# Token groups of 4, 4, 3, 3, 3 instead of 3, 4, 4, 3, 3, with packed small inputs, decay masks a tile at a time and row factors ahead of their spread

## Chip, cores, metric

The kernel runs on one core of one Trainium2 chip. The metric is the device time of one execution in microseconds. Shorter is better. Besides the timed runs there is one execution under the hardware profiler, whose trace gives all rows below.

## What is computed

One layer of a hybrid encoder for 2,048 prompt tokens and 8 x 16 sample tokens, in float32, with a model width of 1,024:

```python
h = rmsnorm(x, norm_mix_pre)
P = h @ w_in                                  # q, k, v, z, b, a, B, C, H
q, k, v = silu(causal_dwconv(P[qkv], 4 taps)); q, k = l2norm(q), l2norm(k)
beta = sigmoid(b);  g = -exp(a_log) * softplus(a + dt_bias)
o = gated_delta_rule(q, k, v, g, beta, S0)    # chunks, a unit-triangular solve in each
o = rmsnorm(o, gdn_norm_w) * silu(z)
y = B * causal_dwconv(C * H, 3 taps)
x = x + rmsnorm(concat(o, y) @ w_o, norm_mix_post)
x = x + rmsnorm(swiglu(rmsnorm(x, norm_ffn_pre)), norm_ffn_post)
```

## The kernel before

The 17 tiles of 128 tokens (tile 16 holds the sample tokens) are worked through in three phases. The first, up to some 905 us of the trace, does the input projection and the delta rule; the second the output projection; the third the feed-forward part. Each float32 product is made of three matmuls: both factors are split into a rounded high part and its remainder (`hi`/`lo` for the input, `wh`/`wl` for a weight).

**Groups and blocks.** In the first phase tiles are taken in five groups (`GROUPS`); a group's columns, 384 or 512, are the width of its matmuls. For each group 28 weight blocks of 128 columns run (`BLOCKS`: k, v, q, z by head, then C, H, B), in the order of `SEQS`. A block is 24 matmuls (L298) into a PSUM bank `dbank`; `finish_block` evacuates it on DVE or ACT (`R`, `sz`, `cs`, `u`, `yo`), and for k, q and v runs a convolution of three taps on DVE (L302). In group 0 each weight block is loaded raw by SP's queue (`wr`, L276), cast on ACT (L277), its remainder taken on DVE (L278) and the pair stored back to memory (`wsplit`, L283); later groups mostly load the stored pair.

**Who sets the order.** TensorE's order is written out by hand: `plan` puts small steps into `events`, at times counted in thirds of a block (3 x place of the block, plus 0, 1 or 2), and the loop over blocks runs those of a third behind its matmuls. The other engines' instructions are ordered by the compiler's scheduler; each engine then runs its own in that order. The numbers of `plan` stand in `PLAN`, by the group's number of tiles, with an entry of its own for group 0: rates, sums, decay, mask, norms, pairs, load, store, the four levels, chunks.

**The delta rule's steps.** `gate_rates`, `gate_sums` and `gate_decay` make the decays; `decay_mask` adds mask and row term for all tiles of a group (L523); `pair_keys` multiplies keys by keys into `AU`. `solve_load` copies the diagonal blocks into `pk` (ACT) and transposes them into `As` (DVE, L569); `solve` makes 31 steps of two DVE instructions each (L578, L580), spread over the plan; `solve_store` transposes the result into `utd` (L585, L586). `level_a` to `level_d` put the block inverses together: level a's matmuls (L600) read `utd`. Then `chunk` takes tile after tile through the state `S`, in four steps.

**The next group's rows.** `x_rows_load` (SP, L228) loads a tile's rows, `x_rows` (ACT, L235) takes their sums of squares; `x_spread` makes the factors (DVE, GpSimd), multiplies them onto a diagonal (DVE, L204) and spreads them over the partitions by a matmul with ones (L207). Group 0 can't wait for that: its first three blocks run on the plain input, and the factors come in at the evacuation (`rb`). Its prologue splits the input (L215, L216), squares it (L874, L875, L878), runs the three blocks, the sums of squares (L888), 16 gate matmuls (L153), then the spread, whose result `rb` is needed by the first evacuation (L309).

**Small inputs.** The identity and ones (`cst`), then the norm vectors (`vec`, 17 numbers a partition) are loaded by ACT's queue at the start; nine more loads (the masks, convolution weights, caches, gate numbers) follow from the same queue behind the first splits.

## Time and profile before

| what | us |
| --- | --- |
| timed runs: 2511.01, 2507.51, 2511.68; median | 2511.01 |
| the profiled execution, its own time | 2506.84 |
| its span, first to last instruction | 2505.1 |
| TensorE busy in it | 2455.0 |
| DVE busy | 1610.7 |
| ACT busy | 1059.6 |

A view by stages gives for each stretch the busy time of each engine, then the granted clock of TensorE (1.00 is full), the busy share of the DMA engines and GB/s. A row of the timeline is start, length, engine (SPq and ACTq are DMA issues), line, operation, out<-in, shapes, count, and in brackets how long the engine had been idle and for whom. A row of groups ends with busy time, mean ns of one, and the idle time ahead of them. A matmul's length covers its way through the array; neighbours overlap, so its cost is the distance from start to start.

### The profile page before, as it was taken

The page shows a single profiled execution, that of the slowest core. Times are in us where ns is not written, and L with a number is a line of the kernel's source. Part 1 is how long each engine was busy: PE and PEld are TensorE (multiplying, and loading weights), DVE is VectorE, ACT ScalarE, POOL GpSimd, SP SyncE. Part 2 cuts the span into 40 slices and gives each one's busy share as a digit, 9 for nine tenths or more (in the row PEclk, how much of TensorE's full clock was granted, in tenths as well). Part 3 has the DMA queues.
Part 4 walks back from the last instruction along what each step waited for, and adds up shares of the span by engine and source line. Part 5 has one row for each costly group of instructions (what it writes and reads, how often), then busy time and mean ns, then how long its engine had stood idle before and what let it go on. Part 6 is the DMA issues. An engine that isn't in the chain of part 4 may idle for free. (4 is left out here: it accounts for less than half of the span.)

```text
span 2505.1 us, 39369 instructions
## 1 busy us (share of the span) xinstructions
PE 2455.0 (98%) x14366; PEld 2247.2 (90%) x14366; DVE 1610.7 (64%) x3032; ACT 1059.6 (42%) x2355; POOL 579.5 (23%) x656
## 2 busy tenths in 40 slices
PE   8999999999999999999999999999999999999997
PEld 7898888889999988889999999999999987887786
DVE  5976645645656555878888754455555564677698
ACT  5556445445435343444443422223333345333343
POOL 1101011011011001135665400000000055455563
PEclk9999999999999999999999999999999999999999
DMA  7855555456667556688876878778898843333365
GB/s 275 310 213 193 211 198 193 175 170 231 242 225 240 200 183 211 209 297 319 292 269 238 290 250 277 264 242 267 291 308 280 259 147 122 93 126 126 128 224 184
DMA packets 282499, 561.91 MB, mean 224 GB/s; under 512 B 26109, under 2 KB 174785, under 8 KB 265025
## 3 DMA queue, kind: packets, MB, share of 16 engines
q1 hardware_dynamic: 161200, 483.52, 56.1%
q10 hardware_dynamic: 121104, 75.88, 9.7%
q8 instruction: 113, 1.85, 0.3%
q14 instruction: 82, 0.66, 0.1%
HBM read 400.62 MB, written 158.70 MB: 223 GB/s over the span
## 5 line engine op out<-in xcount | busy, mean ns | idle before, releaser
L1268 PE MATMUL fbank<-xh,fw 128*128 128x384 f32 (+1 forms) x3696 | 897.8, 326 | 5.9 <-ACT m L1300 2.6
L298 PE MATMUL dbank<-hi,w 128*128 128x384 f32 (+1 forms) x2240 | 672.0, 368 | 8.8 <-ACT w L277 6.2
L1268 PEld LDWEIGHTS fbank<-xh,fw 128*128 128x128 f32 x3696 | 651.0, 188 | 7.5 <-ACT m L1300 3.0
L1268 PE MATMUL fbank<-xl,fw 128*128 128x384 f32 (+1 forms) x1848 | 601.9, 326 | 0.0
L298 PEld LDWEIGHTS dbank<-hi,w 128*128 128x128 f32 x2240 | 416.8, 190 | 47.8 <-ACT w L277 6.2
L1434 PE MATMUL fbank<-dw,as 128*128 128x512 f32 x1884 | 442.6, 393 | 7.5 <-DVE as L1418 2.6
L1434 PEld LDWEIGHTS fbank<-dw,as 128*128 128x128 f32 x1884 | 353.6, 188 | 90.3 <-DVE acc L1393 3.9
L298 PE MATMUL dbank<-lo,w 128*128 128x384 f32 (+1 forms) x1120 | 402.3, 359 | 1.1 <-DVE lo L216 1.1
L1268 PEld LDWEIGHTS fbank<-xl,fw 128*128 128x128 f32 x1848 | 346.9, 188 | 0.0
L1418 POOL TENSOR_TENSOR as<-ar,as 128x256 fp32r<-128x256 f32 (+1 forms) x207 | 186.8, 913 | 226.3 <-ACT as L1415 223.8
L298 PEld LDWEIGHTS dbank<-lo,w 128*128 128x128 f32 x1120 | 212.9, 190 | 18.7 <-DVE lo L216 1.7
L1393 DVE TENSOR_TENSOR acc<-acc,fbank 128x512 f32<-128x512 f32 x248 | 166.3, 682 | 96.1 <-PE fbank L1434 81.9
L1415 ACT CAST as<-ar 128x256 fp32r<-128x256 f32 (+1 forms) x288 | 118.5, 428 | 184.6 <-PE fbank L1434 133.9
L1118 POOL TENSOR_TENSOR dw<-dr,dw 128x512 fp32r<-128x512 f32 x48 | 70.0, 1467 | 520.3 <-ACT dw L1116 520.3
L1243 ACT CAST fw<-rg 128x512 fp32r<-128x512 f32 x124 | 77.4, 624 | 193.8 <-PE fbank L1268 153.1
L302 DVE SCALAR_TENSOR_TENSOR acc<-R,cw,acc 128x384 f32<-128x384 f32 (+2 forms) x180 | 121.6, 678 | 53.2 <-ACT acc L332 44.2
L1313 DVE TENSOR_TENSOR c<-u,fbank 128x384 f32<-128x384 f32 (+1 forms) x66 | 34.9, 529 | 109.9 <-PE fbank L1268 109.9
L1311 ACT ACTIVATE m<-fbank 128x384 f32<-128x384 f32 (+1 forms) x66 | 31.3, 474 | 124.4 <-PE fbank L1268 117.3
L1309 DVE TENSOR_TENSOR m<-m,m 128x384 f32<-128x384 f32 (+1 forms) x44 | 23.1, 525 | 88.8 <-ACT m L1302 88.7
L1244 POOL TENSOR_TENSOR fw<-rg,fw 128x512 fp32r<-128x512 f32 x44 | 71.0, 1614 | 37.0 <-ACT fw L1243 34.7
L324 POOL COPY hist<-R 128x3 f32<-128x3 f32 x60 | 17.0, 283 | 254.5 <-ACT R L307 201.9
L1302 ACT COPY m<-fbank 128x384 f32<-128x384 f32 (+1 forms) x66 | 30.6, 463 | 82.9 <-PE fbank L1268 57.8
(362 smaller groups left out, 3550.6 us busy)
## 6 DMA issues: line engine op xcount, KB each, us to landing
w<-wsplit SPq DMA_DIRECT2D x105, 1024.0 KB, 5.1
fw<-fsplit SPq DMA_DIRECT2D x188, 512.0 KB, 4.7
fsplit<-fw SPq DMA_DIRECT2D x94, 512.0 KB, 3.9
partd<-pt ACTq DMA_DIRECT2D x88, 384.0 KB, 6.6
rg<-in_w_gu SPq DMA_DIRECT2D x62, 512.0 KB, 3.8
wsplit<-w SPq DMA_DIRECT2D x28, 1024.0 KB, 4.9
ar<-partd SPq DMA_DIRECT2D x48, 384.0 KB, 3.3
wr<-in_w_in SPq DMA_DIRECT2D x34, 512.0 KB, 5.8
```

Of the source, the lines that this page charges most:

```text
L298: T.matmul(ps[:, :c], l[:, k, :], r[k][:, :c], start=(k == 0 and r is hi and l is wh), stop=(k == KD - 1 and l is wl))
L302: r = V.scalar_tensor_tensor(acc, raw(d), w[:, d:d + 1], acc, op0=ALU.mult, op1=ALU.add)
L1118: e.tensor_tensor(out=w[1], in0=v, in1=w[0].bitcast(F32), op=ALU.subtract)
L1243: A.copy(w[:, 0], v)
L1244: e.tensor_tensor(out=w[:, 1], in0=v, in1=w[:, 0].bitcast(F32), op=ALU.subtract)
L1268: T.matmul(ps, w_[:, c], b_[k][:, :hw], start=(first and k == 0 and ci == 0), stop=(k == KH - 1 and ci == 2), skip_group_check=not first)
L1311: A.activation(sg0, b1, AF.Silu)
L1313: V.tensor_add(c21, u2, b3)
L1393: V.tensor_add(dst, dst, ps)
L1415: ins = A.copy(a[:, 0, :n], v)
L1418: e.tensor_tensor(out=a[:, 1, :n], in0=v, in1=a[:, 0, :n].bitcast(F32), op=ALU.subtract)
L1434: T.matmul(ps, a[:, x_, q * P:(q + 1) * P], w[y_], start=(start and q == 0 and ci == 0), stop=(q == c - 1 and ci == 2), skip_group_check=True)
```

## The change

Group 0 gets four tiles and group 2 three. `SEQS` takes the v blocks of group 0 earlier, and `PLAN` now has an entry for each group. The convolution, gate and scaling numbers are packed by the host into `vec` (147 numbers a partition), which is loaded first; the masks get a tile of their own and, like the caches, are loaded from SP's queue. Stores of split weights wait until four weight blocks are loaded. The squares of the prologue come behind the second weight block's cast and remainder, two of them on DVE and six on ACT. The factors' diagonal is a step of its own (`diagonal`, `x_factors`), three thirds ahead of the spread; in the prologue the third block's last nine matmuls and eight of the gate matmuls stand ahead of the spread and eight behind it. Rows are loaded every four thirds from 43 on. `decay_mask` and `decay_scale` run a tile at a time. In `level_a` the copies to the diagonals stand behind the two copies that level b reads; from group 1 on four of them are on DVE. Where chunk steps would run far into the next group, the last start is held at its second third.

```diff
-GROUPS = [[0, 1, 2], [3, 4, 5, 6], [7, 8, 9, 10], [11, 12, 16], [13, 14, 15]]
+GROUPS = [[0, 1, 2, 3], [4, 5, 6, 7], [8, 9, 10], [11, 12, 16], [13, 14, 15]]
...
-SEQS = ([0, 12, 1, 13, 2, 14, 3, 15, 8, 16, 9, 17, 10, 18, 11, 19, 4, 20, 5, 21, 6, 7, *range(22, 28)],
+SEQS = ([0, 12, 1, 13, 2, 14, 3, 15, 8, 16, 9, 17, 10, 4, 11, 5, 18, 6, 19, 7, *range(20, 28)],
         [*range(0, 4), *range(8, 12), *range(12, 16), *range(4, 8), *range(16, 28)])
-PLAN = {0: (13, 18, 20, 26, 34, 35, 39, 53, (64, 67, 69, 71), 73),
-        3: (6, 12, 15, 22, 17, 27, 31, 47, (51, 54, 57, 59), 61),
-        4: (6, 12, 15, 20, 17, 24, 29, 42, (45, 48, 50, 52), 55)}
+PLAN = {0: (13, 19, 21, 25, 31, 32, 36, 49, (61, 63, 65, 67), 68),
+        1: (6, 12, 15, 19, 17, 24, 29, 42, (45, 48, 50, 52), 55),
+        2: (6, 12, 15, 21, 17, 27, 31, 47, (52, 55, 58, 60), 62),
+        3: (6, 12, 15, 21, 17, 27, 31, 47, (53, 56, 59, 61), 63),
+        4: (6, 12, 15, 21, 17, 27, 31, 47, (52, 55, 58, 60), 62)}
...
-    cst = const.tile([P, 904], F32, name="cst")
+    cst = const.tile([P, 256], F32, name="cst")
     half_eye = consts[:, 904:]
-    nc.scalar.dma_start(out=cst[:, 0:256], in_=consts[:, 0:256])
-    late = lambda: nc.scalar.dma_start(out=cst[:, 256:], in_=consts[:, 256:904])
-    ident, ones, tri_p, tri_s, blk_s, smask, neg_p, neg_s = (cst[:, a:b] for a, b in CONSTS.values())
-    vec = const.tile([P, 17], F32, name="vec")
+    ident, ones = cst[:, 0:128], cst[:, 128:256]
+    vec = const.tile([P, 147], F32, name="vec")
     nc.scalar.dma_start(out=vec, in_=vecs)
+    nc.scalar.dma_start(out=cst, in_=consts[:, 0:256])
...
+        masks = gp.tile([P, 648], F32, name="masks")
+        tri_p, tri_s, blk_s, smask, neg_p, neg_s = (masks[:, a - 256:b - 256] for a, b in list(CONSTS.values())[2:])
...
-        def spread(r, n):
+        def diagonal(r, n):
+            rg = xbuf()
+            V.tensor_mul(rg[:, :n * P].rearrange("p (t i) -> p t i", t=n), ident.unsqueeze(1).broadcast_to([P, n, P]),
+                         r.unsqueeze(2).broadcast_to([P, n, P]))
+            return rg
+
+        def spread(rg, n):
             c = n * P
-            rg = xbuf()
-            V.tensor_mul(rg[:, :c].rearrange("p (t i) -> p t i", t=n), ident.unsqueeze(1).broadcast_to([P, n, P]),
-                         r.unsqueeze(2).broadcast_to([P, n, P]))
             ps = tbank()
             T.matmul(ps[:, :c], ones, rg[:, :c], start=True, stop=True)
...
-        def x_spread(tiles, nx):
+        def x_factors(tiles, nx):
             n = len(tiles)
             ss = nx["ss"]
             V.tensor_add(ss[:, :n], ss[:, :n], ss[:, MAXT:MAXT + n])
-            nx["rb"] = spread(rstd(small, ss[:, :n], n, 1.0 / D, EPS, "x"), n)
-            nx["hi"], nx["lo"], nx["xk"] = [], [], []
+            nx["rg"] = diagonal(rstd(small, ss[:, :n], n, 1.0 / D, EPS, "x"), n)
+
+        def x_spread(tiles, nx):
+            nx["rb"] = spread(nx["rg"], len(tiles))
...
-                A.copy(wh[:, c], wr[:, c])
-                V.tensor_tensor(out=wl[:, c], in0=wr[:, c], in1=wh[:, c].bitcast(F32), op=ALU.subtract)
+                mark["cast"] = A.copy(wh[:, c], wr[:, c])
+                mark["rest"] = V.tensor_tensor(out=wl[:, c], in0=wr[:, c], in1=wh[:, c].bitcast(F32), op=ALU.subtract)
             wloads.append(wload)
-            while stores:
-                stores.pop()()
+            while stores and len(wloads) > 3:
+                stores.pop(0)()
             if gi == late:
...
-        def gate_matmuls(hi, lo, n):
-            ps = bank()
-            mm3(ps[:16, :n * P], [(wba[:, k, :], v[k][:, :n * P]) for k in range(KD) for v in (hi, lo)])
+        def gate_matmuls(hi, lo, n, ks=range(KD), ps=None):
+            ps = ps or bank()
+            for k in ks:
+                for v in (hi, lo):
+                    T.matmul(ps[:16, :n * P], wba[:, k, :], v[k][:, :n * P], start=(k == 0 and v is hi), stop=(k == KD - 1 and v is lo))
...
-        def decay_mask(g):
-            dt, nG = g["dt"], g["nG"]
+        def decay_mask(g, i):
+            dt, nG, t = g["dt"], g["nG"], g["tiles"][i]
             with tc.issue_after(mark["V"].ins):
-                for i, t in enumerate(g["tiles"]):
-                    for h in range(H):
-                        V.scalar_tensor_tensor(dt[:, i, h, :], dt[:, i, h, :], nG[:, 4 * i + h:4 * i + h + 1],
-                                               neg_s if t == SAMPLE else neg_p, op0=ALU.add, op1=ALU.add)
-            A.activation(dt[:, :g["n"]], dt[:, :g["n"]], AF.Exp)
+                for h in range(H):
+                    V.scalar_tensor_tensor(dt[:, i, h, :], dt[:, i, h, :], nG[:, 4 * i + h:4 * i + h + 1],
+                                           neg_s if t == SAMPLE else neg_p, op0=ALU.add, op1=ALU.add)
+            if i + 1 == g["n"]:
+                A.activation(dt[:, :i + 1], dt[:, :i + 1], AF.Exp)
...
-            nc.sync.dma_start(out=Ts, in_=half_eye)
+            with tc.issue_after(wloads[-1].ins):
+                nc.sync.dma_start(out=Ts, in_=half_eye)
...
         def level_a(g):
             n, npr, ud, td = g["n"], g["npr"], g["ud"], g["td"]
-            for b in range(4):
-                r = slice(32 * b, 32 * b + 32)
-                A.copy(U[r, :n, :, r], ud[r, :n])
             ps = bank()
...
-                A.copy(xs[b:b + 32, :npr, :, 0:32], ps[b:b + 32, 0:128 * npr].rearrange("p (t h c) -> p t h c", t=npr, h=H))
-            for b in range(2):
-                r = slice(32 * b, 32 * b + 32)
-                A.copy(AU[r, :npr, :, r], td[r, :npr])
+                ins = A.copy(xs[b:b + 32, :npr, :, 0:32], ps[b:b + 32, 0:128 * npr].rearrange("p (t h c) -> p t h c", t=npr, h=H))
+            with tc.issue_after(ins.ins):
+                for b in range(2):
+                    r = slice(32 * b, 32 * b + 32)
+                    A.copy(AU[r, :npr, :, r], td[r, :npr])
+                for b in range(4):
+                    r = slice(32 * b, 32 * b + 32)
+                    (V.tensor_copy if g["gi"] else A.copy)(U[r, :n, :, r], ud[r, :n])
...
-            rates, sums, decay, mask, norms, pairs, load, store, levels, chunks = PLAN[n if gi else 0]
+            rates, sums, decay, mask, norms, pairs, load, store, levels, chunks = PLAN[gi]
...
-            at(mask, decay_mask, g)
             at(norms, key_norms, g)
             for i in range(n):
-                at(pairs - 1, decay_scale, g, i)
+                at(mask + i, decay_mask, g, i)
+                at(pairs + 3 * (i // 2) + i % 2 - 1, decay_scale, g, i)
                 at(pairs + 3 * (i // 2), pair_keys, g, i)
-                at((33 if gi else 50) + 3 * (i // 2), pair_queries, g, i)
+                at((33 if gi else 52) + 3 * (i // 2), pair_queries, g, i)
...
-                t += 6
+                t = min(t + 6, 3 * len(BLOCKS) + 1)
...
-                    at(44 + 3 * i, x_rows_load, tiles, i, nx)
-                    at(47 + 3 * i - (i < m - 1), x_rows, i, nx)
-                at(48 + 3 * m, x_spread, tiles, nx)
+                    at(43 + 4 * i, x_rows_load, tiles, i, nx)
+                    at(46 + 4 * i, x_rows, i, nx)
+                b = 47 + 4 * m + (0 if gi else 3)
+                at(b - 3, x_factors, tiles, nx)
+                at(b, x_spread, tiles, nx)
...
-            sq = xbuf()
             if k % 2:
-                V.tensor_mul(sq[:, :c], raw, raw)
-                V.tensor_add(sq[:, :c], sq[:, :c], sqs[-1][:, :c])
-                sqs[-1] = sq
+                sq = cp.tile([P, W1], F32, tag="cs" if k < 4 else "vraw", name="sq", bufs=2 if k < 4 else NKV)
             else:
-                A.activation(sq[:, :c], raw, AF.Square)
+                sq = xbuf()
                 sqs.append(sq)
+            with tc.issue_after(mark["cast"].ins), tc.issue_after(mark["rest"].ins):
+                if k in (1, 3):
+                    V.tensor_mul(sq[:, :c], raw, raw)
+                else:
+                    A.activation(sq[:, :c], raw, AF.Square)
+                if k % 2:
+                    squared = V.tensor_add(sqs[-1][:, :c], sqs[-1][:, :c], sq[:, :c])
...
-        for q in range(1, NPD):
-            matmuls(firsts[q], pending[q][1:], hi, lo, c, range(KD))
+        matmuls(firsts[1], pending[1][1:], hi, lo, c, range(KD))
+        matmuls(firsts[2], pending[2][1:], hi, lo, c, range(5))
...
-        started = mark["hi"].ins
-        inputs = ExitStack()
-        inputs.enter_context(tc.issue_after(started))
-        late()
-        cw = gp.tile([P, 12, 4], F32, name="cw")
-        scw = gp.tile([P, 4, 3], F32, name="scw")
-        nc.scalar.dma_start(out=cw, in_=conv_w)
-        nc.scalar.dma_start(out=scw, in_=sc_w)
...
+        rg = diagonal(rx, n)
+        matmuls(firsts[2], pending[2][1:], hi, lo, c, range(5, KD))
+        cw = vec[:, 17:65].rearrange("p (c d) -> p c d", d=4)
...
-        nc.scalar.dma_start(out=cch, in_=cache_c)
-        nc.scalar.dma_start(out=sch, in_=cache_s)
...
-        gps = gate_matmuls(hi, lo, n)
-        rb = spread(rx, n)
+        gps = gate_matmuls(hi, lo, n, range(0, 4))
+        rb = spread(rg, n)
+        gate_matmuls(hi, lo, n, range(4, KD), gps)
...
+        def constants():
+            with tc.issue_after(wloads[-1].ins):
+                nc.sync.dma_start(out=masks, in_=consts[:, 256:904])
+
+        events = {9: [constants]}
+
+        def caches():
+            with tc.issue_after(wloads[-1].ins):
+                nc.sync.dma_start(out=cch, in_=cache_c)
+                nc.sync.dma_start(out=sch, in_=cache_s)
+
         for gi, tiles in enumerate(GROUPS):
+            if gi == 1:
+                events.setdefault(30, []).append(caches)
...
-                            wait = 10 - n if gi else 7 if BLOCKS[j][0] == "v" else 13
+                            kind = BLOCKS[j][0]
+                            wait = (7 if kind == "v" else 13) if not gi else 13 - n if kind == "q" else 10 - n
```

The built order shows three places. First ACT's, at the start; `xk<-U` is a square of the input, `hi` the first split, and what a row waits for stands behind it (DMAHW: a landed load). Before, and then now:

```order
L132 DMA cst<-in_consts 128x256
L136 DMA vec<-in_vecs 128x17
L878 ACT_TABLE_LOAD
L878 ACTIVATE xk<-U 128x384 [waits DMAHW1_49]
L215 ACTIVATE hi<-U,vec 128x384 [waits DMAHW2_49]
```

```order
L131 DMA vec<-in_vecs 128x147
L132 DMA cst<-in_consts 128x256
L216 ACT_TABLE_LOAD [waits DMAHW1_49]
L216 ACTIVATE hi<-U,vec 128x512 [waits DMAHW0_49]
L281 CAST w_222<-wr 128x512 [waits DMAHW3_49]
```

The vector's load went ahead of the constants', the square went away from the front, and the table load now stands behind the wait for the vector.

Second TensorE's, from the end of the third block on to the fourth; `gbank<-..wba` are the gate matmuls, `tbank<-xk,cst` is the spread. Before:

```order
L153 MATMUL gbank<-hi,wba 16x384
L153 MATMUL gbank<-lo,wba 16x384
L153 MATMUL gbank<-hi,wba 16x384
L153 MATMUL gbank<-lo,wba 16x384
L207 MATMUL tbank<-xk,cst 128x384 [waits DVE_49]
L298 MATMUL dbank<-hi,w_459 128x384 [waits DVE_49,Activation_49]
```

Now:

```order
L440 MATMUL gbank<-lo,wba 16x512
L208 MATMUL tbank<-xk,cst 128x512 [waits DVE_49]
L440 MATMUL gbank<-hi,wba 16x512
L440 MATMUL gbank<-lo,wba 16x512
L440 MATMUL gbank<-hi,wba 16x512
L440 MATMUL gbank<-lo,wba 16x512
L440 MATMUL gbank<-hi,wba 16x512
L440 MATMUL gbank<-lo,wba 16x512
L440 MATMUL gbank<-hi,wba 16x512
L440 MATMUL gbank<-lo,wba 16x512
L302 MATMUL dbank<-hi,w_446 128x512 [waits DVE_49,Activation_49]
```

The spread moved ahead of eight gate matmuls.

Third DVE's, in group 0 just ahead of level a; `R` is the evacuation of a block, `w` a weight remainder, `acc` a tap, `pr` and `Ts` the solve. Before:

```order
L309 TENSOR_TENSOR R<-dbank,rb 128x384 [waits PE_49]
L580 TENSOR_TENSOR Ts<-Ts,pr 128x3x15 [waits DVE_49]
L578 TENSOR_TENSOR pr<-As,Ts 128x30 [waits DVE_49]
L580 TENSOR_TENSOR Ts<-Ts,pr 128x2x15 [waits DVE_49]
L278 TENSOR_TENSOR w_1499<-wr,w_1499 128x1024 [waits DMAHW6_49,DMAHW0_49,Activation_49]
L578 TENSOR_TENSOR pr<-As,Ts 128x16 [waits DVE_49]
L302 SCALAR_TENSOR_TENSOR acc<-R,cw,acc 128x384 [waits Activation_49]
L580 TENSOR_TENSOR Ts<-Ts,pr 128x16 [waits DVE_49]
L302 SCALAR_TENSOR_TENSOR acc<-R,cw,acc 128x384 [waits DVE_49]
L585 STREAM_TRANSPOSE utd<-Ts 128x32x16 [waits DVE_49]
```

Now:

```order
L313 TENSOR_TENSOR R<-dbank,rb 128x512 [waits PE_49]
L585 TENSOR_TENSOR pr<-As,Ts 128x45 [waits DVE_49]
L587 TENSOR_TENSOR Ts<-Ts,pr 128x3x15 [waits DVE_49]
L282 TENSOR_TENSOR w_1484<-wr,w_1484 128x1024 [waits DMAHW4_49,Activation_49]
L585 TENSOR_TENSOR pr<-As,Ts 128x30 [waits DVE_49]
L306 SCALAR_TENSOR_TENSOR acc<-R,vec,acc 128x512 [waits Activation_49]
L587 TENSOR_TENSOR Ts<-Ts,pr 128x2x15 [waits DVE_49]
L306 SCALAR_TENSOR_TENSOR acc<-R,vec,acc 128x512 [waits DVE_49]
L585 TENSOR_TENSOR pr<-As,Ts 128x16 [waits DVE_49]
L306 SCALAR_TENSOR_TENSOR acc<-R,vec,acc 128x512 [waits DVE_49]
L587 TENSOR_TENSOR Ts<-Ts,pr 128x16 [waits DVE_49]
L592 STREAM_TRANSPOSE utd<-Ts 128x32x16 [waits DVE_49]
```

The evacuation, the remainder and the taps that stand between the last solve steps stayed, with one tap more ahead of the transposition.

51 lines of the change are left out of this document (22 added, 29 removed).

## Prediction

> **What bounds the kernel now.** I read the page's head first, then the busy time by stage, then who made TensorE wait, and last the rows around the long waits.
>
> ```profile
> span 2505.1 us, 39369 instructions
> ...
> 0.00:160.00 160.00, 140.97 (x963) 134.08 (x964) 121.95 (x261) 91.79 (x157) 17.90 (x45) 0.97 0.79 285
> 160.00:905.00 745.00, 740.75 (x4931) 663.39 (x4931) 423.34 (x1056) 364.14 (x866) 74.89 (x169) 1.00 0.58 204
> 905.00:2505.10 1600.10, 1573.31 (x8476) 1449.76 (x8474) 1065.45 (x1717) 603.66 (x1334) 486.69 (x442) 1.00 0.69 228
> ```
>
> The columns of the stages are length, then busy time of PE, weight load, DVE, ACT and POOL, then granted clock. TensorE is busy almost throughout: it idles 19.0 us in the first 160 us, 4.3 us in the rest of the first phase, 26.8 us behind it. The built order has 13,290 matmuls before and 13,294 now (four more one-column ones), and behind the first phase the order of every engine is the same. So the change can only move the 23.3 us of idle time ahead of 905 us, and clock lost around it. Those 19.0 us, and group 4's entry, are:
>
> ```profile
> PE dbank L298 <- ACT w L277: 6.2, 1, 6.2
> PE tbank L207 <- DVE xk L204: 4.9, 1, 4.9
> PE gbank L481 <- DVE gg L473: 1.9, 1, 1.9
> PE dbank L298 <- DVE R L309: 1.7, 1, 1.7
> PE gbank L600 <- DVE utd L585: 1.5, 1, 1.5
> PE tbank L343 <- ACT kT L336: 1.2, 1, 1.2
> PE dbank L298 <- DVE lo L216: 1.1, 1, 1.1
> ...
> PE tbank L207 <- DVE xk L204: 1.1, 1, 1.1
> ...
> PE gbank L600 <- DVE utd L585: 0.5, 1, 0.5
> ```
>
> (us in total, times, longest; the last two rows are from 160 us on.) Two of these waits also cost clock:
>
> ```profile
> 112.23 0.94 SPq L228 DMA_DIRECT2D xt<-in_x  x2
> 118.97 0.61 ACT L235 ACTIVATE xt<-xt 128x512 f32<-128x512 f32 x1
> 122.92 2.04 PE L207 MATMUL tbank<-xk,cst 128*128 128x512 f32 x2 [4.90 <-DVE xk L204]
> 125.08 0.52 PE L298 MATMUL dbank<-lo,w 128*128 128x384 f32 x1
> 126.04 0.52 PE L298 MATMUL dbank<-lo,w 128*128 128x384 f32 x1
> 128.20 0.34 PE L298 MATMUL dbank<-lo,w 128*128 128x384 f32 x1
> 128.72 0.33 PE L298 MATMUL dbank<-lo,w 128*128 128x384 f32 x1
> 133.87 1.04 PE L600 MATMUL gbank<-utd,AU 32*32 32x32 f32 x48 [1.52 <-DVE utd L585]
> 135.33 0.52 PE L298 MATMUL dbank<-lo,w 128*128 128x384 f32 x1
> 136.29 0.52 PE L298 MATMUL dbank<-lo,w 128*128 128x384 f32 x1
> ```
>
> Three 384-wide matmuls take 0.52 us (128.20 to 128.72), but 0.96 behind the spread wait (125.08 to 126.04) and behind the level-a wait (135.33 to 136.29). From 122.9 to 128 TensorE does the two spread passes and some nine matmuls, about 2.7 us of work, so 2.3 us are lost; from 134.8 to 138 some ten matmuls, 1.5 us lost.
>
> **The work is the same.** The groups of four only move from places 1 and 2 to places 0 and 1. Third stands below for a third of a block in the plan. A 512-wide matmul costs per column what a 384-wide one does:
>
> ```profile
> 246.95 0.39 PE L298 MATMUL dbank<-lo,w 128*128 128x512 f32 x1
> 247.64 0.39 PE L298 MATMUL dbank<-lo,w 128*128 128x512 f32 x1
> ```
>
> 0.69 us for three against 0.52, which is 4/3. So group 0 grows by what group 2 shrinks: zero. What changes is the time that the other engines have per block there: the weight cast and its remainder are fixed per block, while a block grows from 24 x 0.173 = 4.2 us to 24 x 0.231 = 5.5 us.
>
> **The start.**
>
> ```profile
> 1.66 1.28 ACT L878 ACT_TABLE_LOAD   x1 [1.66 <-PEq L1581]
> 5.05 0.61 ACT L215 ACTIVATE hi<-U,vec 128x384 fp32r<-128x384 f32 x1 [1.03 <-DMA vec<-in_vecs]
> ...
> cst<-in_consts ACTq DMA_DIRECT2D x1, 128.0 KB, 2.9
> cw<-in_conv_w ACTq DMA_DIRECT2D x1, 24.0 KB, 7.2
> vec<-in_vecs ACTq DMA_DIRECT2D x1, 8.5 KB, 3.8
> ```
>
> The vector now goes first (0.73 us instead of 1.20) but the first table load stands behind the wait for it. Landing in 2.9 us, as the first issue does now, gives a first split at 0.73 + 2.9 + 1.28 = 4.9 us; in 3.8, as the vector does now, 5.8; against 5.05. I take the middle, 0.3 us later, since it is now the first issue but nine times as large. With 7.2 us, the row of a small load under traffic, it would be 9.2: 4.2 us later. Against that the squares leave DVE, so the 1.1 us wait for lo mostly goes; but the matmuls are slow until some 15 us (0.32 us each), so only about half of what is won counts: +0.6. Nine loads leave ACT's queue; the cast that they held back cost TensorE 0.3 us, the last of the minor waits. Three of them (the masks, two caches) go to SP's, each right behind a weight load, many blocks before their first use: nothing, and if a weight load behind them came late, about the 0.5 us that an issue takes there. Start: +0.3 - 0.3 + 0.3 = **+0.3** (-4.2 to +1.2). Of the packed load the Trainium skill says (DMA: Bandwidth & Descriptors, Specifications) that a transfer wants at least 512 B for line rate; the rows go from 68 to 588 B, so by that page the estimate would be the earlier landing, half a microsecond better. No row here has the new shape.
>
> **The first evacuation.**
>
> ```profile
> 30.60 0.48 ACT L209 COPY rb<-tbank 128x384 f32<-128x384 f32 x1 [2.21 <-PE tbank L207]
> 31.11 0.56 DVE L926 TENSOR_TENSOR rb<-rb 128x384 f32<-128x384 f32 x1 [0.99 <-ACT rb L209]
> 31.59 0.55 DVE L309 TENSOR_TENSOR R<-dbank,rb 128x384 f32<-128x384 f32 x1
> ```
>
> From the spread's end to TensorE's next block are 1.7 us with no matmul placed between. At 4/3 of the width that is some 2.2 us, and eight 512-wide gate matmuls now stand there: 8 x 0.231 = 1.85. Wait 0.4: **+1.3** (1.0 to 1.7).
>
> **The first transposition and the gates.** The distance to the kT transposition is the same in blocks, so 4/3 longer; before it DVE now does six taps in a row where a weight remainder stood among them. **+1.2** (0 to 1.2). The sums stand six thirds of a block behind the rates instead of five: 6 x 1.85 = 11.1 us instead of 5 x 1.39 = 7.0, 4 us more against a wait of 1.9, for a chain of small instructions that hardly grows: **+1.9** (1 to 1.9).
>
> **The spread.** The last rows were issued at third 53, and the spread stood at 60: 7 x 1.39 = 10 us, and it was 4.9 late. Now 55 and 66: 11 x 1.85 = 20 us. It goes, and its slow clock with it: 4.9 + 2.3 = **+7.2**. What is late next is level a.
>
> **Level a.** DVE is what was late in this stretch:
>
> ```profile
> 89.80 2.10 DVE L569 STREAM_TRANSPOSE As<-pk 128x1024 f32<-128x1024 f32 x1 [0.15 <-ACT pk L567]
> 102.56 1.22 DVE L278 TENSOR_TENSOR w<-wr,w 128x1024 fp32r<-128x1024 f32 x1 [2.25 <-ACT w L277]
> 129.27 0.56 DVE L309 TENSOR_TENSOR R<-dbank,rb 128x384 f32<-128x384 f32 x1
> 132.76 1.06 DVE L585 STREAM_TRANSPOSE utd<-Ts 128x512 f32<-128x512 f32 x1
> ...
> L278 DVE TENSOR_TENSOR w<-wr,w 128x1024 fp32r<-128x1024 f32 x25 | 30.6, 1222 | 13.3 <-ACT w L277 13.3
> L302 DVE SCALAR_TENSOR_TENSOR acc<-R,cw,acc 128x384 f32<-128x384 f32 x36 | 21.7, 611 | 3.0 <-ACT acc L334 2.8
> ...
> L302 DVE SCALAR_TENSOR_TENSOR acc<-R,cw,acc 128x512 f32<-128x512 f32 x60 | 45.0, 750 | 31.4 <-ACT acc L332 30.3
> ```
>
> From As to the end of the first utd DVE took 44.0 us. TensorE reached level a 44.1 us after As, of which 4.9 + 1.5 + 2.3 were waits and slow clock: 35.4 us of work. So DVE was 8.7 us late, and that is what these losses are. Now: 25 thirds lie between loading and level a in both, so TensorE has 35.4 x 4/3 = 47.2 us. By the order DVE does the same 8 remainders and the same solve there, 18 taps of 0.75 instead of 14 of 0.61 (+5.0), six R of 0.69 instead of four of 0.55 (+1.9) and some +0.5 elsewhere: 44.0 + 7.4 = 51.4, or 49.2 without the 2.25 us for a late load. DVE is late by 2.0 to 4.2. From below the tail bounds it: R to utd took 4.55 us, now one more tap and wider tiles, 5.6, against 18 matmuls, 4.2: 1.4. I take a wait of 3.0 (1.4 to 4.5) instead of 1.5, and a slow clock worth 2.0 instead of 1.5: **-2.0** (0 to -4.5).
> The Trainium skill (TensorE: Matmul & The Clock Gate, What's actually happening) puts the fall to half speed behind an idle window of about 3.4 us. The 4.9 us wait agrees and the 1.7 us one at 32 us cost no clock, but the 1.52 us one was followed by 0.96 us per three. By the page 3.0 us would cost no clock, and the time would be an estimated 2 us less.
>
> **Later groups.** In group 3 the factors now come three thirds ahead of the spread and level a two thirds later: +1.4 of the 1.6 us. Sixteen copies into U go from ACT to DVE, some 0.55 us each by the 384-wide rows; DVE is busy 423 of 745 us there, and level a's wanted copies stand ahead of them, so nothing; if that cover is gone, about 2 us where one stands ahead of a remainder or a scaling. Group 2's new table is near the one under which group 4 ran without a wait. I allow 0.8 for new waits: **+0.6** (-1.5 to +1.6).
>
> **Sum.** 0.3 + 1.3 + 1.2 + 1.9 + 7.2 - 2.0 + 0.6 = 10.5 us. The profiled execution took 2506.8 us for a span of 2505.1: it would take 2496.3. The median of the runs, 2511.0, is 4.2 above the profiled one, so I forecast 2500.5 for it. With the bounds of the terms the forecast's own range is 2495 to 2506.
>
> **Rivals.**
> 1. *The lateness moves to level a.* If DVE keeps idling for loads and casts as at 102.56, it is some 7 us late there: 4 us more of waiting and 0.5 of clock, 2505. For it: DVE's remaining margin is only arithmetic. Against: a block has a third more time for the same load. 0.14.
> 2. *Group 0's tail turns DVE-bound: slower.* Behind level a three chunk steps fall into the group instead of two, and the fourth follows one third behind the third. The seven blocks left are 42 us with their transpositions. If DVE stays late there as it was before level a (44.0 for 35.4, 24%), that is 10 us, with two slow stretches (3.8) and some 3 more at level a: 17 us, 6 more than is won, 2517. It decides from 10.5 us of lateness. Against: groups of four ran so before with under 1 us of waits. 0.11.
> 3. *The packed vector lands late* (7.2 us): 4.5 us less won, 2505. 0.08.
> 4. *It doesn't do what it says*: the waits are met again in groups 1 to 4 with their new tables, 10 us in all, 2511. 0.07.
>
> **Chances.** The forecast has 0.60. A measurement here tells about 0.2%, 5 us, from no change. Faster by more: 0.60, with 0.6 of rival 1 (0.08) and 0.7 of rival 3 (0.06): 0.74. Slower: most of rival 2, 0.10. Same: 0.16. Eight times in ten: 2492 (all terms at their better end, with the runs' own spread of 4) to 2511 (rival 4).
>
> **What would show it.** No wait at the spread of group 0 and no half clock there; a level-a wait of 1.4 to 4.5 us on utd, with three matmuls at 1.28 us behind it; the first matmul at 6 to 7 us; under 1 us at the first R and at gg; phases behind 900 us unchanged but earlier. A first matmul at 10 us, a wait over 6 us at level a, or waits for r and S at the end of group 0 would make it wrong.

## The result, and the profile after

| | before | after |
| --- | --- | --- |
| timed runs, median of 5 each, us | 2511.4 (2507.51 to 2514.95) | 2499.33 (2498.35 to 2501.09) |
| ratio, 95% interval | | 0.9954 (0.9942 to 0.9965) |
| profiled execution, its own time | 2506.84 | 2499.33 |
| its span | 2505.1 | 2497.4 |
| last projection matmul ends, in the trace | 902.9 | 893.0 |

The change makes the kernel 0.46% faster; the forecast was 2500.5 us with a range of 2492 to 2511. Timed once more beside other kernels, the changed kernel stood at 0.9962 (0.9949 to 0.9976), 2500.92 us against 2511.61.

Stages of the changed kernel, with the columns of the stage view shown for before (length, busy PE, weight load, DVE, ACT, POOL, granted clock, DMA share, GB/s):

```profile
0.00:180.00 180.00, 168.14 (x1024) 136.46 (x1025) 128.72 (x253) 100.70 (x160) 20.35 (x42) 0.99 0.70 244
180.00:900.00 720.00, 715.63 (x4895) 662.03 (x4894) 426.75 (x1082) 351.03 (x848) 74.28 (x172) 1.00 0.61 214
900.00:2497.40 1597.40, 1570.88 (x8459) 1447.91 (x8458) 1062.22 (x1711) 599.68 (x1329) 484.76 (x442) 0.99 0.70 227
```

TensorE idles 11.9 us in the first 180 us, where it idled 19.0 us in 160 before. The rest of the first phase idles 4.4 us, as before. The waits of TensorE in the first 200 us (total, times, longest):

```profile
PE dbank L302 <- ACT w L281: 6.4, 1, 6.4
PE gbank L604 <- issue: 2.3, 1, 2.3
PE gbank L551 <- DVE AU L552: 1.2, 1, 1.2
PE dbank L302 <- DVE R L313: 0.9, 1, 0.9
PE dbank L302 <- ACT hi L216: 0.9, 1, 0.9
PE obank L702 <- DVE o L725: 0.9, 1, 0.9
```

Gone are the waits at the spread (4.9), for gg (1.9) and for kT (1.2). The wait at level a (L604) grew from 1.5 to 2.3, the one at the first evacuation (L313) fell from 1.7 to 0.9, and two are new: the pair keys wait 1.2 us for AU, a chunk 0.9 for o. The row of level a says "issue", but the timeline of DVE and then of TensorE at that place names the releaser:

```profile
149.66 1.08 DVE L592 STREAM_TRANSPOSE utd<-Ts 128x512 f32<-128x512 f32 x1
```

```profile
150.85 1.20 PE L604 MATMUL gbank<-utd,AU 32*32 32x32 f32 x64 [2.27 <-issue]
...
153.21 0.63 PE L302 MATMUL dbank<-lo,w 128*128 128x512 f32 x1
...
154.49 0.63 PE L302 MATMUL dbank<-lo,w 128*128 128x512 f32 x1
```

DVE's transposition ends at 150.74, and level a starts at 150.85. Behind it three matmuls take 1.28 us (153.21 to 154.49) instead of 0.69. The clock in stretches of 5 us (length, busy PE, granted clock, DMA share, GB/s) shows the same:

```profile
150.00:155.00 5.00, 4.15 (x73) 0.78 0.66 215
155.00:160.00 5.00, 5.00 (x143) 0.88 0.01 3
```

Lost are 5 x 0.22 + 5 x 0.12 = 1.7 us.

### The profile page after: what moved, and what is told of

Same layout as the page of the kernel before. It is cut to its first block, busy times and chain, and to the rows that moved or that the text cites. A ratio compares the mean times of both kernels' runs of the same rounds, so it can differ in the third digit from the quotient of the medians.

```text
span 2497.4 us, 39376 instructions
## 1 busy us (share of the span) xinstructions
PE 2454.7 (98%) x14374; PEld 2246.4 (90%) x14374; DVE 1617.7 (65%) x3045; ACT 1051.4 (42%) x2337; POOL 579.4 (23%) x656
## 5 line engine op out<-in xcount | busy, mean ns | idle before, releaser
L1284 PE MATMUL fbank<-xh,fw 128*128 128x384 f32 (+1 forms) x3696 | 899.6, 326 | 5.3 <-ACT m L1316 2.5
L1284 PEld LDWEIGHTS fbank<-xh,fw 128*128 128x128 f32 x3696 | 652.3, 188 | 6.9 <-ACT m L1316 2.8
L1284 PE MATMUL fbank<-xl,fw 128*128 128x384 f32 (+1 forms) x1848 | 602.4, 326 | 0.0
L302 PEld LDWEIGHTS dbank<-hi,w 128*128 128x128 f32 x2240 | 414.4, 189 | 48.9 <-ACT w L281 6.4
L1284 PEld LDWEIGHTS fbank<-xl,fw 128*128 128x128 f32 x1848 | 347.5, 188 | 0.0
L306 DVE SCALAR_TENSOR_TENSOR acc<-R,vec,acc 128x512 f32<-128x512 f32 (+2 forms) x180 | 121.4, 676 | 46.6 <-ACT acc L336 40.5
```

What stands on the lines that cost most here:

```text
L302: T.matmul(ps[:, :c], l[:, k, :], r[k][:, :c], start=(k == 0 and r is hi and l is wh), stop=(k == KD - 1 and l is wl))
L306: r = V.scalar_tensor_tensor(acc, raw(d), w[:, d:d + 1], acc, op0=ALU.mult, op1=ALU.add)
L1284: T.matmul(ps, w_[:, c], b_[k][:, :hw], start=(first and k == 0 and ci == 0), stop=(k == KH - 1 and ci == 2), skip_group_check=not first)
```

## Experiments

Twelve runs. Beside times and waits, one sum is used: the time **lost** in a group. For each two neighbouring matmuls of the first phase it is the distance of their starts, less the lower quartile of that distance for the same two shapes over all profiles; so it holds idle time and slow clock together.

| lost, us, one profile each | group 0 | 1 | 2 | 3 | 4 | sum |
| --- | --- | --- | --- | --- | --- | --- |
| before / b_again | 26.6 / 28.6 | 7.6 / 7.9 | 5.7 / 5.7 | 8.2 / 8.8 | 5.8 / 5.7 | 53.8 / 56.7 |
| after / a_again | 17.7 / 16.5 | 5.6 / 5.6 | 4.8 / 4.8 | 5.8 / 5.8 | 7.4 / 10.9 | 41.3 / 43.7 |
| b_groups | 22.3 | 5.5 | 8.5 | 10.4 | 8.7 | 55.4 |
| b_groups_q | 22.7 | 7.1 | 5.8 | 8.7 | 7.1 | 51.3 |
| a_oldgroups | 25.9 | 10.0 | 5.8 | 6.8 | 8.5 | 57.1 |
| a_undo2 | 25.1 | 5.6 | 4.8 | 5.8 | 7.6 | 49.0 |
| a_levels_ok | 11.3 | 6.0 | 4.8 | 5.8 | 9.3 | 37.3 |
| a_best | 14.8 | 6.0 | 4.7 | 5.8 | 6.4 | 37.6 |

From before to after the sum falls by 12.5 and 13.0 us, but the time from the first matmul to the last projection only by 10.0 and 10.5. The lower quartiles themselves add up to some 2.5 us more in the changed kernel; 0.9 of it are eight more records of one-column matmuls at 0.11 us. So a difference of 2 to 3 us between the sums of the two kernels is not read.

**b_again and a_again: how steady is a profile?** Both kernels unchanged.

> The kernel before, unchanged, profiled once more. Its first profiled execution took 2506.8 us where its timed runs have a median of 2511.4; the changed kernel's took 2499.3, its own median. If the first profile of before was simply a fast execution, this one lies nearer to 2511 and the 4 us more stand behind 905 us, in phases whose order the change does not touch: output projection above 198.6 us and feed-forward above 921.1 and 466.5. If instead the later phases are steady from run to run, they repeat 198.6, 921.1 and 466.5 within 0.5 us, and the 3.2 us that the changed kernel takes longer there are an effect of the change. In both cases group 0 shows the spread wait of 4.9 us, the level-a wait of 1.5 and the half clock behind them within 0.5 us.

> The changed kernel, unchanged, profiled once more and timed beside the two next ones. Its ratio to before should fall inside the first interval, 0.9942 to 0.9965. The first profile showed idle time and slow clock of 17.7 us in group 0; a profile of the kernel before moved by 2 us there between two executions at the same waits, so 15 to 20 us are expected here, with the wait at level a within 0.5 us of 2.3 and the stretch from the first matmul of the output projection to the end within 1.5 us of 1603.8 us.

b_again took 2509.0 us. Its waits lie within 1.2 us of the first profile's (the spread 3.7, level a 2.1), more than the 0.5 us expected, one of 1.8 at level c is new, and the half clock stands behind the spread and level c, not behind level a. So the first profile of before lay below its median, but its later phases repeated: output projection 199.7 and 199.7 us from its first matmul to the first of the feed-forward part, and that part 921.2 and 921.2. a_again's profiled execution took 2506.8 us although its timed median is 2500.9: its first phase ended 10.1 us ahead of b_again's (895.3 against 905.4), as after's ended 9.9 ahead of before's, but its feed-forward part took 926.3 us where after's took 922.2; TensorE's waits for m there (L1284) were 7.5 us together, against 5.3. So the expectation for the later phases failed on the side of the changed kernel: one execution varies by some 4 us behind the first phase. Phase one is the place to compare, and there the two pairs agree on 10 us. The output projection takes 202.0 and 202.1 us in the changed kernel, 2.3 more in both: its first matmul follows the last one of the first phase sooner, and waits for wol and mh come behind it instead. At the first matmul of the feed-forward part the lead is therefore 8.7 and 8.8 us (1104.33 against 1095.66, 1106.90 against 1098.10).

**b_spread66: does the lateness move?** The kernel before, with only the spread of group 0 later:

```diff
-                at(48 + 3 * m, x_spread, tiles, nx)
+                b = 48 + 3 * m + (0 if gi else 6)
+                at(b, x_spread, tiles, nx)
...
-                        at(ts[k] + 3, x_norm, tiles, k, nx)
+                        at(max(ts[k], b) + 3, x_norm, tiles, k, nx)
```

> The kernel before with one edit: group 0's spread stands at third 66 instead of 60 (the normalisations behind it at 69 or later); rows are loaded when they were. Theory 1 (DVE is 8.7 us late at level a whatever stands ahead, 44.0 us of DVE's stretch against 35.4 of TensorE's work): the spread wait of 4.9 us and the 2.3 us of half clock go, TensorE reaches level a about 7 us sooner, and the wait for utd there grows from 1.5 to about 8.7 us, so the time stays within 2 us of before, ratio 0.999 to 1.001. Theory 2 (the late rows were the loss, and DVE waited for the stalled TensorE's evacuations there): the level-a wait stays at 1.5 to 3 us and the time falls by about 6 us, ratio 0.9975.

2512.3 us, ratio 1.0005 (0.9997 to 1.0014). The first row of its waits:

```profile
PE gbank L600 <- DVE utd L585: 9.2, 1, 9.2
```

No wait at the spread is left, and level a waits 9.2 us, where theory 1 said 8.7. DVE's stretch from As to utd took 43.7 us, against 44.0 before: it is DVE's own time, not time spent waiting for a stalled TensorE. The later spread by itself is worth nothing.

**a_oldgroups: all but the groups.** The changed kernel with groups of 3, 4, 4, 3, 3 (and group 1's numbers for group 2, which has four tiles now):

```diff
-GROUPS = [[0, 1, 2, 3], [4, 5, 6, 7], [8, 9, 10], [11, 12, 16], [13, 14, 15]]
+GROUPS = [[0, 1, 2], [3, 4, 5, 6], [7, 8, 9, 10], [11, 12, 16], [13, 14, 15]]
```

> The changed kernel with the old groups of 3, 4, 4, 3, 3 (group 2, now of four tiles, gets group 1's numbers), all else as changed: the spread 11 thirds behind the last row. Theory 1: 11 x 1.39 = 15.3 us cover the 14.6 that the rows need, so no spread wait and no half clock there, but level a stands as many thirds behind the loading as before, at 384 columns: DVE is late there by the 8.7 us that the spread no longer covers, and waits for utd of 7 to 9 us take the place. First evacuation under 0.5 us, gg about 0.6. Won in all 3 to 5 us, ratio 0.998 to 0.999. Theory 2: the level-a wait stays under 3 us and the kernel is as fast as the changed one, ratio 0.9955.

2519.0 us, ratio 1.0031 (1.0016 to 1.0045): slower than before, where a gain of 3 to 5 us was expected. The wait went where theory 1 put it, and is longer than the 7 to 9 us that it gave:

```profile
PE gbank L604 <- issue: 10.3, 1, 10.3
```

DVE took 48.9 us from As to utd, and TensorE was there 10.3 us ahead of it. In group 1 some 2 us more are lost, two stored weights coming late (3.5 us of waits). The profiled execution, 2513.9 us, was the fastest but one of eight (up to 2523.9), so about 5 us of this kernel's median are not in its trace and stay unexplained.

**b_groups and b_groups_q: the groups alone.** The kernel before with the new groups, block order, table, third for the queries (52) and hold of the last chunk; then with one rule more:

```diff
-                            wait = 10 - n if gi else 7 if BLOCKS[j][0] == "v" else 13
+                            kind = BLOCKS[j][0]
+                            wait = (7 if kind == "v" else 13) if not gi else 13 - n if kind == "q" else 10 - n
```

> The kernel before with groups of 4, 4, 3, 3, 3 and the new block order, table of numbers and hold of the last chunk; prologue, small inputs, row loading (last row issued at third 53, spread at 60), masks and level a's copies as before. Theory 1 (the wider group 0 gives the other engines a third more time per block, and that carries the change): the waits of 1.2 at kT and 1.9 at gg go; the spread stands 7 x 1.85 = 13 us behind its last row where 9.7 + 4.9 = 14.6 were needed, so it waits about 1.6 us, with up to 2 us of half clock; the level-a wait is 1 to 4 us; the first evacuation still waits some 2.2 us. Some 5 to 6 us of the 12 are won, ratio 0.998. Theory 2 (what is loaded sooner carries it): 0 to 2 us are won, ratio 0.999 to 1.000, and the spread waits as before, over 4 us.

> The run with the kernel before and groups of 4, 4, 3, 3, 3, with one rule more of the change: a q block's transpositions stand 13 - n thirds behind the block instead of 10 - n from group 1 on. Without it six waits for qT, 6.4 us together, stood in the later groups. Theory 1 (that rule was missing, and the rest of what group 0 won is there): the qT waits fall under 1 us and the time from 2514 to about 2507, ratio 0.9985. Theory 2 (the later groups lose for another cause, such as row loading or level a's copies on ACT): the qT waits go, but others come in their place, and the time stays over 2511, ratio 1.000 or above.

b_groups: 2514.05 us, ratio 1.0010 (1.0002 to 1.0019); neither theory's time. Its waits, the first 200 us and then the rest of the first phase:

```profile
PE gbank L547 <- DVE AU L548: 3.0, 1, 3.0
PE dbank L300 <- DVE R L311: 2.1, 1, 2.1
PE gbank L602 <- DVE utd L587: 1.3, 1, 1.3
```

```profile
PE tbank L345 <- ACT qT L338: 6.4, 6, 2.3
PE tbank L209 <- DVE xk L206: 1.3, 1, 1.3
```

In group 0 it is as theory 1 says and better: no wait at the spread although it stands at third 60 and rows are loaded when they were, 2.1 us at the first evacuation, 1.3 at level a; 4 to 6 us less lost there than before. But the pair keys wait 3.0 us for AU, and the groups behind lose 5 to 6 us more, the largest part of it six waits for qT. b_groups_q, with the rule for q blocks, has no wait for qT over 0.3 us and takes 2508.22 us, ratio 0.9990 (0.9981 to 0.9999), near the 2507 of theory 1. So that one line of the diff carries some 5 us in this order of groups (1.0010 against 0.9990, each against before in its own batch). What b_groups_q still loses more than the changed kernel is 10 us: 5 in group 0, 3 in group 3, 2 elsewhere.

**a_rows_old: the rows loaded sooner.** The changed kernel with before's times for rows and spread:

```diff
-                    at(43 + 4 * i, x_rows_load, tiles, i, nx)
-                    at(46 + 4 * i, x_rows, i, nx)
-                b = 47 + 4 * m + (0 if gi else 3)
+                    at(44 + 3 * i, x_rows_load, tiles, i, nx)
+                    at(47 + 3 * i - (i < m - 1), x_rows, i, nx)
+                b = 48 + 3 * m
```

> The changed kernel with rows loaded when before loaded them (44 + 3i, sums of squares at 47 + 3i or one less, the spread at 48 + 3m: third 60 in group 0), groups and all else as changed. Theory 1 (the wider blocks alone give the rows their time: the spread at 60 did not wait in the run with groups alone): no wait for xk in group 0 and the time of the changed kernel within 2 us, ratio 0.995 to 0.9963. Theory 2 (the later spread is needed: 7 x 1.85 = 13 us against the 14.6 that the rows took): a wait for xk of 1.6 us with 2 us of half clock behind it, ratio 0.997.

2501.43 us, ratio 0.9964 (0.9952 to 0.9977), no wait for xk in group 0, level a 1.9 us: theory 1. With a wider group 0 the new times for rows are worth at most about 2 us, inside the intervals; a wait of 0.6 for xk behind 200 us is all that came.

**a_undo2: masks a tile at a time, and the spread among the gate matmuls.** Both undone in the changed kernel:

```diff
-        gps = gate_matmuls(hi, lo, n, range(0, 4))
+        gps = gate_matmuls(hi, lo, n)
         rb = spread(rg, n)
-        gate_matmuls(hi, lo, n, range(4, KD), gps)
...
-                at(mask + i, decay_mask, g, i)
-                at(pairs + 3 * (i // 2) + i % 2 - 1, decay_scale, g, i)
+                at(mask, decay_mask, g, i)
+                at(pairs - 1, decay_scale, g, i)
```

> The changed kernel with two parts undone: the prologue's spread stands behind all 16 gate matmuls, and masks and scalings of a group's tiles are all put at one third, as before. Theory 1 (these two account for what the run with groups and block order alone still lost in group 0): the first R wait grows from 0.9 to about 2.3 us (there 2.1), the wait for AU at the pair keys from 1.2 to 2.4 (there 2.4 to 3.0) with 1.5 us of slow clock behind it, 4 us in all, ratio 0.997. Rival (the wait for AU is set by the plan's numbers and the first R by the factors, not by these parts): both waits stay within 0.4 us and the time within 1 us, ratio 0.9955.

2506.1 us, ratio 0.9982 (0.9973 to 0.9990): 5 us slower than the changed kernel beside it. Its waits:

```profile
PE gbank L551 <- DVE AU L552: 2.4, 1, 2.4
...
PE dbank L302 <- DVE R L313: 2.1, 1, 2.1
```

Both came back to the size that they have in b_groups_q, and in this profile each is followed by slow clock:

```profile
40.00:45.00 5.00, 5.00 (x16) 0.66 0.13 52
...
95.00:100.00 5.00, 2.65 (x14) 0.82 0.77 289
```

So these two parts together are worth about 5 us, once the groups are wide; which of them how much was not run. The 1.7 us of slow clock behind the first evacuation are no fixed part of it: b_groups_q has the same wait of 2.1 us and 1.00 behind it.

**a_levels2 and a_levels_ok: level a later.** The changed kernel, with group 0's entry first at (63, 65, 67, 69), 70, then:

```diff
-PLAN = {0: (13, 19, 21, 25, 31, 32, 36, 49, (61, 63, 65, 67), 68),
+PLAN = {0: (13, 19, 21, 25, 31, 32, 36, 49, (63, 65, 67, 69), 69),
```

> The changed kernel with group 0's four levels at 63, 65, 67, 69 and its chunks from 70, two thirds of a block later (2 x 1.85 = 3.7 us of TensorE's work). Theory 1 (DVE ends utd a fixed 2.3 us after TensorE gets to level a, and the half clock behind it, some 2 us, belongs to that wait): both go, 4 us less than the changed kernel's 2499, so 2495, ratio 0.9938. Rival (DVE's order follows the plan: the evacuation and taps of two thirds more come ahead of the last solve steps, so it stays late): a wait for utd of 1 to 2 us stays, with half clock behind it, and less than 2 us are won. Second rival (level b to d or the chunks become late instead): new waits of over 1 us behind 155 us, ratio 0.9955 or above.

> The changed kernel with group 0's levels at 63, 65, 67, 69 and its chunks from 69 (69, 75, 81, 85), so that each tile still starts from the state that the tile ahead of it leaves. In the run with chunks from 70 the level-a wait and the slow clock behind it were gone (6 us less lost in group 0) and a wait of 1.9 us for o appeared in group 1. Theory 1 (level a was the last place where DVE's lateness shows, and the wait for o came from the last two chunks being crowded together): no wait for utd, no wait for o over 1 us, 4 to 6 us less than the changed kernel, ratio 0.9935. Rival (the lateness goes on to the chunks, whose second step now stands two thirds behind level d instead of three): a wait at the chunks of 1 to 2 us, and 2 to 4 us won, ratio 0.9945.

In a_levels2 chunks start at 70, 76, 82 and 85, so the last tile's first step (85) stands ahead of the state update of the tile before (86) and reads a state one tile old; it doesn't compute the layer, and only its times are read. It took 2495.5 us, ratio 0.9947 (0.9934 to 0.9960), without a wait at level a, and with 1.9 us for o in group 1. a_levels_ok took 2496.28 us, ratio 0.9941 (0.9927 to 0.9954), 4.6 us under the changed kernel, with neither wait. DVE and TensorE at level a in it:

```profile
148.71 1.20 DVE L592 STREAM_TRANSPOSE utd<-Ts 128x512 f32<-128x512 f32 x1
...
150.55 0.39 PE L302 MATMUL dbank<-hi,w 128*128 128x512 f32 x1
...
150.87 1.20 PE L604 MATMUL gbank<-utd,AU 32*32 32x32 f32 x64
```

Level a starts at 150.87, where it started at 150.85, but two thirds of a block more have been done by then, TensorE comes from a matmul, and the clock stays at 1.00. DVE is done 1.0 us ahead. The ratio lies between the two that were expected, but the waits decide for theory 1 in a_levels_ok. In a_levels2 the second rival has its part: the wait for o.

**a_table and a_best: the start, and a weight in group 4.** The first edit puts ACT's table load ahead of the first input's landing; a_best has it together with a_levels_ok's table and a later load of the decay rows in group 4.

```diff
+    warm = const.tile([P, 1], F32, name="warm")
+    V.memset(warm, 0.0)
+    A.activation(warm, warm, AF.Copy, scale=warm)
...
+            if gi == 4:
+                at(decay + 2, decay_rows, g)
```

(`decay_rows` is the last line of `gate_decay`, the load of dt, behind the newest weight load in every group; group 4's masks start at 22.)

> The changed kernel with one tiny activation on a cleared tile ahead of the first split, so that ACT's table load (1.28 us, which stood behind the wait for the first input tile, 3.79 to 5.09 us) runs before that tile lands; one number more is written, nothing else changes. If the table load sets the start, the first split begins at about 3.8 us and the first matmul at 5.1 to 5.4 us instead of 6.37; with the first matmuls slow, half of that or so counts in the time. If the first weight's load or cast sets it, the first matmul stays at 6 us or later.

> The changed kernel with group 0's levels two thirds later and its chunks from 69 (as in the run that won most), the table load ahead of the first split, and in group 4 the load of the decay rows (dt) behind the next stored weight on SP's queue, as the kernel before had it (masks from third 22). In the changed kernel that load stands ahead of the weight, SP waits up to 5.6 us there for the rows to be written, the two weights behind it land 9 to 10 us after their issue instead of 5 to 6, and TensorE waits 1.6 to 3.6 us for a weight at 780 us. Theory 1 (that order makes the weight late): the wait for a stored weight in group 4 is gone, idle time and slow clock of group 4 fall from 7.4 to 10.9 back to about 5.7 us, the first matmul is at 5.4 us, and the time falls 2 to 4 us below the run with the levels alone, to 2492 to 2494, ratio 0.9925 to 0.9935. Rival (traffic on the DMA engines makes the weight late, whatever the order): the wait stays at 1.5 to 3.6 us in group 4, ratio 0.994.

a_table's first matmul started at 5.36 us instead of 6.37, as expected, but the 25th started at 14.95, inside the 14.6 to 15.9 of the two profiles without the edit. The one execution took 2502.7 us, and one execution can't show a second: nothing is seen of it in the time. In the trace full clock begins at 12.6 us, against 12.8 and 11.6 without the edit. What SP's queue waits for, between 755 and 790 us, in after and then in a_best, where no wait for grow is left:

```profile
SPq L522 <- DMA grow<-rw: 5.9, 1, 5.9
```

```profile
SPq L871 <- DVE ot L688: 6.3, 1, 6.3
```

and TensorE's waits behind 200 us in a_again and in a_best:

```profile
PE dbank L302 <- DMA w<-wsplit: 3.6, 1, 3.6
```

```profile
PE dbank L305 <- DMA w<-wsplit: 0.6, 1, 0.6
```

(The first profile of the changed kernel puts its wait of 1.6 us there down to ACT, but it ends at 781.5 us, 0.1 us behind the landing of a weight that was issued at 773.6.) In the changed kernel the load of dt stands ahead of a weight load in SP's queue; in before it stood behind that weight, and SP waited 1.2 us. Put back, TensorE's wait fell to 0.6 us, where the seven other profiles of the changed kernel and its edits in wide groups have 1.5 to 3.6. But it was not SP's hold that made the weight late: in a_best SP stands 6.3 us at another step ahead of the same weight, and the weight is issued 41.0 us into group 4 in both (773.6 against 770.1 us in the trace). What the order changed is whose transfer goes first. The weight now behind dt still takes 9.4 us to land (772.0 to 781.5), but it is needed a block later. So theory 1 holds for the order, and its step by way of SP's waiting does not.

a_best took 2492.94 us, ratio 0.9927 (0.9914 to 0.9941): 17 us under the kernel before, the fastest of all. Group 4 loses 6.4 us, near the 5.7 expected. Against a_levels_ok (0.9941) the gain lies within the intervals, and the sums of lost time, 37.6 and 37.3, don't show it: the profile of a_best has 3.4 us of slow clock in group 0 that the other has not.

## Why the prediction was right, point by point

The sum was 10.5 us; the first phase ends 9.9 us earlier in one pair of profiles and 10.1 in the other. Ahead of the feed-forward part 8.7 and 8.8 us of it are left, since the output projection, which the prediction put at no change, starts 10.9 and 11.2 us earlier but takes 2.3 us longer. The medians differ by 12.1 and 10.7; the 2 to 3 us beyond the traces stand in no pair of profiles. So the whole was right, and mostly for its reasons, but some terms missed and made up for each other, partly by luck.

- **The spread, +7.2: right.** No wait, no half clock. The step behind it was only half right: I gave the credit to the rows (55 and 66 instead of 53 and 60). a_rows_old and b_groups show that wider blocks alone do it.
- **DVE 8.7 us late before level a: right,** and the heart of the matter. b_spread66 found 9.2, a_oldgroups 10.3. This is why moving the spread wins nothing by itself. With 4/3 of the time per block DVE is 1.3 to 2.3 us late instead (b_groups, after).
- **Level a, -2.0: right in kind, too dark.** Wait 2.3 instead of 3.0 (1.4 to 4.5), slow clock 1.7 instead of 2.0, so -1.0. DVE's stretch was put at 49.2 to 51.4 us and took 49.5; TensorE's work at 47.2 and took 150.85 - 2.27 - 101.23 = 47.4.
- **kT and gg, +1.2 and +1.9: right,** both gone. What the prediction did not name is the wait for AU in their place, 1.2 and 0.7 us. Masks a tile at a time had no term at all; without them, and with the spread behind all gate matmuls (a_undo2), it is 2.4 us and slow clock.
- **First evacuation, +1.3: mis-sized.** Forecast wait 0.4, measured 0.9 and 1.6. The bound of 2.2 us without the new order was right (2.1 in b_groups and a_undo2).
- **Start, +0.3:** the first matmul came at 6.37 and 6.27 (before 6.22 and 5.86); the wait for lo is gone in both profiles of the changed kernel, a wait of 0.9 for hi is in one of them. About nothing, within the scatter. The packed vector landed in 3.2 and 3.1 us, between the 2.9 and 3.8 that were weighed. The table load stood behind the wait for the first input tile (3.79 us), not, as said, for the vector (landed at 3.9). And the term was added up wrongly: +0.6 for lo, -0.3 and +0.3 give +0.6, not +0.3.
- **Later groups, +0.6:** the 1.6 us in group 3 went as said, but a weight is late in group 4 by 1.6 to 3.6 us. I had looked at DVE and ACT for new waits there, not at the order of SP's queue. Net about 0 to -2. Groups 1 and 2 lose some 3 us less by the table, about the margin given there; no term was for them.
- **From profile to median: wrong.** I carried over 4.2 us, the distance of before's profiled execution from its median. In the changed kernel's first profile that distance is 0, and in its second -5.9. The profiled execution was forecast 3.0 us too low (2496.3 against 2499.3), and the two errors cancelled by luck. The forecast's own range doesn't follow either: the bounds of the terms add up to 2496 to 2512, not 2495 to 2506.

Of the rivals, the 7 us of lateness at level a did not come, the chunks of group 0 waited 0.9 us for o and not 10, the packed vector was not late, and but for the weight in group 4 the waits did not come back in later groups.

The parts don't add. Against the kernel before of the same runs the groups with their order and the rule for q are worth 2 us, the rest without the groups costs 8, and both together win 11. The block order and the table are in all three. From the waits it looks as if the rest smooths what the wider group makes the next limit, and has nothing to smooth where DVE is 10 us late. That is argued, not shown: the table's numbers for group 0 were made for four tiles, and some 5 of the 8 us stand in no trace.

## What to carry to other kernels

Where one engine is late at a deadline, a wait ahead of it hides part of that lateness: compare the late engine's stretch with the bound engine's work up to the last deadline before a wait is counted as a gain. Give such a stretch more time per step (here a wider group while the weights are cast) or move the deadline, and look again for what is next. When steps move in a plan, read the order of every DMA queue ahead of the loads that the bound engine will wait for, and ask there whose transfer comes first, not only who holds up the issue.

## What was not expected of the hardware

Slow clock comes in stretches of 3.41 us at half rate, 1.7 us lost in each, and not at every wait. Ahead of 900 us the granted clock of every trace changes only at multiples of 3.41 us from its first record, where full clock begins (in after that is at 12.82 us, and the fall at 152.76 is 41 stretches later). The 14 profiles have 29 falls there. In each, the stretch of 3.41 us just ahead of the fall was idle, or ran matmuls of at most 64 columns, for 1.8 us or more. So the place of a wait on this grid counts as well as its length. At the first evacuation of a_undo2 a wait of 2.1 us lies in one stretch, and the clock falls; in a_oldgroups one of 2.7 us for vraw (88.5 to 91.2) lies half in one and half in the next, and it stays (length, busy PE, granted clock, DMA share, GB/s):

```profile
36.80:40.21 3.41, 1.32 (x5) 1.00 0.96 298
40.21:43.62 3.41, 3.41 (x10) 0.50 0.13 50
```

```profile
86.37:89.78 3.41, 2.06 (x12) 1.00 0.99 363
89.78:93.20 3.42, 2.03 (x13) 1.00 0.92 373
93.20:96.61 3.41, 3.41 (x23) 1.00 1.00 323
```

At level a the 2.1 us of b_again are cut in two as well, and cost no clock, while the 1.5 us of before lie in one stretch with the small matmuls behind them. The first record stands at 10.8 to 15.3 us, differently in each execution of one kernel, so which wait costs clock is partly chance. Where the limit lies was not settled: with some 1.9 us of idle time in a stretch the clock fell in a_levels_ok (776 us) and did not in b_groups (39 us).

The clock also falls where TensorE waits for nothing, at 25 to 35 us, in 8 of the 14 profiles, among them a_best (5 us stretches, granted clock behind the count):

```profile
20.00:25.00 5.00, 5.00 (x27) 1.00 0.97 326
25.00:30.00 5.00, 5.00 (x31) 0.71 1.02 417
30.00:35.00 5.00, 5.00 (x15) 0.60 0.85 331
```

That is 3.4 us lost there, while a_levels_ok, with the same order from the first blocks up to group 4, shows 1.00. The sums of squares, matmuls of one column, run there, from 24.4 us on in a_best: 2.7 us of them lie in the one stretch up to 27.1. In after they are cut into 1.7 and 1.8 us, and the clock stays. The Trainium skill (TensorE: Matmul & The Clock Gate, What's actually happening) has the clock fall behind an idle window of some 3.4 us; the 2.27 us at level a, with small matmuls behind it, were enough here.
